# A hybrid RG-LRU and gating layer: an earlier end, statistics and splits spread over the boundaries, and three kinds of instruction pinned in order

## The chip, the cores and the metric

The kernel runs on one core of a Trainium2 chip. The metric is device time in microseconds (us), the median over runs; lower is better. Five engines with instruction lines of their own work on it: PE (matrix multiply), DVE (vector), ACT (scalar and activation), POOL and SP. DMA transfers are issued from SP's, ACT's and POOL's lines. An engine takes its instructions strictly in order.

## The reference, cut to what matters

```python
z = rms_norm(x, pre_g)                       # 2048 prompt tokens + 64 sample tokens, width 2048
proj = z @ w_in                              # width 5 * 1024: xr, gr, u, v, gs
xc, new_buf = causal_depthwise_conv(xr, ...) # 4 taps, with carried state for the samples
hr, h_last = rg_lru(xc, ...)                 # two gates per head (128 x 128), then h = a*h + b over time
br = hr * silu(gr)
v  = rms_norm(gelu(v), sgu_g)
bs = chunk_spatial_gating(gelu(u), v, w_s, b_s) * silu(gs)   # mixing inside chunks of 128 tokens
out = concat(br, bs) @ w_out                 # 2048 x 2048
y   = x + rms_norm(out, post_g)
```

All in float32. Outputs are y for prompt and samples, the new conv and recurrence states, and the normalised v of the samples.

## The kernel before, in words

**Groups.** The tokens are worked on in four groups of 512 prompt tokens; group 0 carries the 64 sample tokens with it (576 columns). Every product is taken as three passes of a split number: `split` (L155) makes a high half on ACT and a low half on DVE, and PE adds high·high, high·low and low·high. So each weight piece (128 x 1024) goes through three stations: a load `wraw` on SP's line (L176), its high half `wh` on ACT (L184), its low half `wl` on DVE (L192).

**Group 0** runs plain products, job by job: xr and gr for the recurrence (with conv, gates and scan, `lru0`, in between), v, gs and u, then sixteen out jobs, each a 128-row block of w_out. Its order on the engines is set by a scheduler; `later` (`tc.keep_in_program_order`, L92) ties one instruction to the place where the program hands it in. `at(job, f)` hands a task in behind a job. Beside it, in group 0, POOL's line loads quadrants of the weights (`load_quadrants`, L229) and `make_sums` (L236) forms four sums per unit (P1, P3, P2, P4), which are stored to memory: 16 units "c" of w_in on DVE, four of w_v and eight of w_or (from w_out) on POOL. At the end of the u jobs, `cat` is loaded again from memory as `cb` (L340) and split into c0h and c0l for the out jobs.

**Groups 1 to 3** use those sums for a scheme of seven products in place of eight: PROD names the weight side (B11, P4, B21, P2, P1, P3, B22), ACTS the activation side (A11, A22, A12, E, D1, D3, F, each with a high and a low half, `z_hi` on ACT and `z_lo` on DVE; `pre` forms E, D1, D3 and F before the split). A `quad` is two weight units for each of the seven products (14 steps), a `wide` four units (28 steps). Each group has four quads for xr and gr (G, 56 steps), one wide for v (V, 28), four quads for gs and u (U, 56) and two wides for out (O and R2, 28 each): 196 steps a group. Here the order is written by hand: `at2(s, f)` puts a task at step s, `early` ahead of it, `late` behind its matmuls. Loads run LOADS = 6 steps ahead, halves LOOK = 3, with three buffers each.

**Around the boundaries.** The next group's input x is loaded (`stat_load`), squared and summed on ACT (`stat_sum`), turned into 1/rms (`stat_rstd`), spread over the partitions by PE (`stat_spread` makes xd and the matmul nsx, L639; `stat_take` copies it back) and applied (`z_norm`). The finished group's output is normalised, x is added by an accumulating DMA on POOL's line, and stored (`finish_*`). For groups 1 and 2 four of eight quarters are still in the chip's memory and four are loaded again (`finish_load`, tile fo). At the very end the last group is done in halves of 256 rows: `last_rstd`, `last_gain`, then `last_scale` (ACT scales, a DMA accumulates into x, SP stores) for half 1 or `last_both` (DVE scales and adds, ACT stores) for half 0.

Of the kernel before, what the change touches and what calls it, by code (L numbers as in the profile page):

```python
# [46 lines left out]
PROD = ["B11", "P4", "B21", "P2", "P1", "P3", "B22"]  # L47
ACTS = ["A11", "A22", "A12", "E", "D1", "D3", "F"]


@with_exitstack
def hybrid_layer(ctx: ExitStack, tc: tile.TileContext, a):
# [183 lines left out]
    def make_sums(unit):  # L236
        nm = "_".join(str(x) for x in unit)
        t = state.pop(("quad", unit))

        def put(k, x):  # L240
            sums[unit, k] = hp.tile([P, W], F32, name=f"{k}_{nm}")
            side.dma_start(sums[unit, k], x)

        eng = nc.vector if unit[0] == "c" else nc.gpsimd
        eng.tensor_add(t["B11"], t["B11"], t["B12"])
        put("P1", t["B11"])
        eng.tensor_add(t["B12"], t["B12"], t["B22"])
# [402 lines left out]
    def z_norm(g, j, rows=(0, 1)):  # L650
        x = state["R", g, j]
        for i in rows:
            nc.vector.scalar_tensor_tensor(x[:, i, :TP], x[:, i, :TP], col(C_PRE, 2 * j + i), state["rB", g],
                                           op0=ALU.mult, op1=ALU.mult)

# [62 lines left out]

    def evac(r, bk, tmp, put):

        k = PROD[r]
        if k == "B11":
            nc.scalar.activation(tmp["U"], bk["a"], AF.Copy)
        elif k == "B21":
            put(0, 0, bk["a"], None, None)
        elif k == "P2":
            nc.vector.tensor_sub(tmp["U"], bk["b"], tmp["U"])
        elif k == "P1":
            nc.scalar.activation(tmp["D"], bk["d"], AF.Copy)
# [14 lines left out]
    def quad(g, name, unit_pairs, put):  # L744
# [21 lines left out]
    def wide(g, name, kind, q, put):  # L766

        bks, tmp = {}, {}

        def mm(r, u, key):  # L770
            b = BANK[PROD[r]]
            if u == 0 and b not in bks:
                bks[b] = [bank(f"w{g}{name}{b}{i}") for i in range(2)]
            mm_wide(key, r, u, bks[b])

        def take_product(r, i):
            if i == 0 and r == 0:
                tmp["U"] = dbl(f"U{g}{name}")
            elif i == 0 and PROD[r] == "P1":
                tmp["D"] = dbl(f"D{g}{name}")  # L780
            evac(r, {x: y[i] for x, y in bks.items()}, {x: y[:, i, :TP] for x, y in tmp.items()},
                 lambda n, half, *args: put(n, half, i, tmp, *args))

        for r, k in enumerate(PROD):
            for u in range(4):
                steps2.append((mm, r, u, (g, kind, q, u, k)))
            for i in range(2):
                at_once = k == "P1" or (k == "B22" and g == NG - 1 and name == "o1")
                early[len(steps2) + (0 if at_once else i)].append((take_product, r, i))

# [238 lines left out]

    def last_scale(half, qq):  # L1030

        o, x = state["og", half, qq], state["lx", half, qq]
        for i in range(2):
            nc.scalar.activation(o[:, i], o[:, i], AF.Copy, scale=state["lors", half][:, i:i + 1])
        side.dma_start(x, o, accum_op=ALU.add)
        nc.sync.dma_start(rows("y", NG - 1, half, qq), x)

    def last_both(half, qq):
# [3 lines left out]
        for i in range(2):  # L1042
            nc.vector.scalar_tensor_tensor(x[:, i], o[:, i], state["lors", half][:, i:i + 1], x[:, i],
                                           op0=ALU.mult, op1=ALU.add)
            nc.scalar.dma_start(y[:, i], x[:, i])

# [33 lines left out]
    for g in range(1, NG):  # L1080
# [98 lines left out]

    for c in ACTS:  # L1180
        for j in range(4):
            if c == "E":
                pre(("R", 1), "D3", j)
            if c in ("E", "D1", "F"):
                pre(("R", 1), c, j)
            z_hi(("R", 1), c, j)
            z_lo(("R", 1), c, j)

    def combine(key, c, j, s):

        at2(s, z_hi, key, c, j)
        at2(s + 1, z_lo, key, c, j)

    for g in range(1, NG):
        G = len(steps2)
        V, U, O, R2 = G + 56, G + 84, G + 140, G + 168
        for n, us in enumerate(XG):
            quad(g, f"xg{n}", us, put_xg(g, 2 * n))  # L1200
# [205 lines left out]
```

## Time and profile before

| | us |
|---|---|
| median of 3 runs (lowest to highest) | 2599.7 (2595.08 to 2603.26) |
| profiled execution, its own time | 2598.45 |
| its span in the trace | 2596.8 |
| PE busy | 2502.2 (96%) |
| DVE, ACT, POOL busy | 1737.8, 1398.3, 468.0 |
| mean granted PE clock | 0.988 |

In the rows below, a timeline line has start, duration, engine, source line, operation, out<-in, shape, a count, and in brackets the idle time before it with what ended it. L numbers are lines of the kernel before; in the changed kernel the same code stands 3 or more lines further down. Group 0 lasts to about 804 us, group 1 to about 1402, group 2 to about 1998. A tile's buffer numbers are left out in the profile (pB11c for all units "c").

### The profile page before, as it was taken

To read this page: it belongs to the slowest core of one execution; us is meant where nothing else is said; L and a number is where in the kernel's file an instruction comes from. 1 tells how busy PE (TensorE), PEld (TensorE's weight loads), DVE (VectorE), ACT (ScalarE), POOL (GpSimd) and SP (SyncE) were. 2 spreads that over 40 slices of the span, in tenths; PEclk is the share of its full clock that TensorE was granted. 3 is DMA by queue.
4 is the path that set the end of the run, shared out by engine and by line. 5 is a ranking of instruction groups with operands and counts; after the bars stand their busy time and mean duration, and the time that the engine had idled before them with its cause. 6 is when DMAs were issued, how large, how long until landed. Compare 5 with 4: busy or idle time off the path is not lost.

```text
span 2596.8 us, 41550 instructions
## 1 busy us (share of the span) xinstructions
PE 2502.2 (96%) x16710; PEld 2303.2 (89%) x16710; DVE 1737.8 (67%) x2236; ACT 1398.3 (54%) x1787; POOL 468.0 (18%) x552
## 2 busy tenths in 40 slices
PE   7989999999998999999999899999999899999996
PEld 6989789999997998899888898899878898899884
DVE  7776165554357786756788586656789587656865
ACT  5445332232144677555765577645756577645653
POOL 4331025954721200100100200000100200000000
PEclk9999999999999999999999999999999999999998
DMA  6995389975764855856876955555876955555676
GB/s 227 327 329 207 103 315 327 366 264 199 279 210 150 283 189 171 250 180 191 276 247 206 298 194 163 183 182 189 263 255 202 316 181 177 179 181 177 191 265 184
DMA packets 168673, 589.21 MB, mean 227 GB/s; under 512 B 19216, under 2 KB 19776, under 8 KB 168480
## 3 DMA queue, kind: packets, MB, share of 16 engines
q1 hardware_dynamic: 106544, 377.06, 43.7%
q0 software_dynamic: 60784, 207.40, 23.9%
q8 instruction: 130, 2.13, 0.3%
q10 hardware_dynamic: 1152, 2.10, 0.2%
q14 instruction: 63, 0.52, 0.1%
HBM read 494.92 MB, written 89.47 MB: 225 GB/s over the span
## 4 chain that ended last, share of the span: by engine, by line
PE 70%; DMA 9%; DVE 8%; ACT 5%; issue 5%; POOL 3%; SPq 0%; DVEq 0%; ACTq 0%; POOLq 0%
PE gm0v L378 4%; PE gm0gs L367 4%; PE gm0u L367 4%; PE gm0out L367 3%; PE gm0gr L367 3%; PE gm0xr L367 2%; DVE wl_c_B L192 1%; PE g L854 1%; PE sp L556 1%; DMA pB12c<-w_in 1%; DMA wraw_c_P<-P_c 1%; PE w3vd L713 1%; PE w2o1a L713 1%; PE w1o1d L713 1%; PE w3o1a L713 1%
## 5 line engine op out<-in xcount | busy, mean ns | idle before, releaser
L184 ACT ACTIVATE wh_c_P<-wraw_c_P 128x1024 fp32r<-128x1024 f32 x192 | 203.1, 1059 | 270.6 <-DMA wraw_c_P<-P_c 89.7
L192 DVE TENSOR_TENSOR wl_c_P<-wraw_c_P,wh_c_P 128x1024 fp32r<-128x1024 f32 x192 | 234.4, 1222 | 114.7 <-ACT wh_c_P L184 114.6
L192 DVE TENSOR_TENSOR wl_c_B<-wraw_c_B,wh_c_B 128x1024 fp32r<-128x1024 f32 x144 | 175.4, 1221 | 85.4 <-ACT wh_c_B L184 85.4
L184 ACT ACTIVATE wh_c_B<-wraw_c_B 128x1024 fp32r<-128x1024 f32 x144 | 152.0, 1057 | 140.3 <-DMA wraw_c_B<-w_in 41.6
L192 DVE TENSOR_TENSOR wl_w_or_P<-wraw_w_or_P,wh_w_or_P 128x1024 fp32r<-128x1024 f32 x96 | 117.4, 1223 | 44.5 <-ACT wh_w_or_P L184 44.1
L184 ACT ACTIVATE wh_w_or_P<-wraw_w_or_P 128x1024 fp32r<-128x1024 f32 x96 | 101.6, 1058 | 81.9 <-DMA wraw_w_or_P<-P_w_or 26.0
L184 ACT ACTIVATE wh_w_or_B<-wraw_w_or_B 128x1024 fp32r<-128x1024 f32 x72 | 76.2, 1059 | 80.4 <-DMA wraw_w_or_B<-w_or 24.5
L367 PE MATMUL gm0out<-c0l,wh_out 128*128 128x288 f32 x512 | 111.7, 299 | 1.0 <-DVE c0l L158 0.8
L367 PE MATMUL gm0out<-c0h,wl_out 128*128 128x288 f32 x512 | 110.5, 297 | 0.5 <-DVE wl_out L192 0.4
L367 PE MATMUL gm0out<-c0h,wh_out 128*128 128x288 f32 x512 | 110.4, 297 | 0.0
L192 DVE TENSOR_TENSOR wl_w_or_B<-wraw_w_or_B,wh_w_or_B 128x1024 fp32r<-128x1024 f32 x72 | 88.0, 1222 | 32.8 <-ACT wh_w_or_B L184 32.3
L617 POOL DMA_DIRECT2D xs<-xt x24 | 12.8, 536 | 504.7 <-ACT wh_c_P L184 257.3
L192 DVE TENSOR_TENSOR wl_out<-wraw_out,wh_out 128x1024 fp32r<-128x1024 f32 x32 | 48.2, 1507 | 64.4 <-ACT wh_out L184 64.4
L184 ACT ACTIVATE wh_out<-wraw_out 128x1024 fp32r<-128x1024 f32 x32 | 33.7, 1056 | 97.8 <-PE gm0out L367 66.7
L367 PEld LDWEIGHTS gm0out<-c0l,wh_out 128*128 128x128 f32 x512 | 82.4, 189 | 2.3 <-DVE c0l L158 1.7
L367 PEld LDWEIGHTS gm0out<-c0h,wl_out 128*128 128x128 f32 x512 | 82.4, 189 | 1.5 <-DVE wl_out L192 1.0
L367 PEld LDWEIGHTS gm0out<-c0h,wh_out 128*128 128x128 f32 x512 | 82.2, 189 | 0.1
L192 DVE TENSOR_TENSOR wl_w_v_P<-wraw_w_v_P,wh_w_v_P 128x1024 fp32r<-128x1024 f32 x48 | 58.5, 1222 | 28.5 <-ACT wh_w_v_P L184 28.5
L184 ACT ACTIVATE wh_w_v_P<-wraw_w_v_P 128x1024 fp32r<-128x1024 f32 x48 | 49.9, 1054 | 47.0 <-DMA wraw_w_v_P<-P_w_v 35.0
L367 PE MATMUL gm0gr<-z0h,wl_gr 128*128 128x288 f32 x256 | 56.9, 304 | 7.1 <-DVE wl_gr L192 7.1
L367 PE MATMUL gm0xr<-z0h,wh_xr 128*128 128x288 f32 x256 | 56.6, 302 | 7.2 <-ACT wh_xr L184 5.1
L378 PE MATMUL gm0v<-wh_v,z0l 128*128 128x512 f32 (+1 forms) x160 | 63.3, 396 | 0.0
(1612 smaller groups left out, 8610.8 us busy)
## 6 DMA issues: line engine op xcount, KB each, us to landing
wraw_c_P<-P_c SPq DMA_DIRECT2D x192, 512.0 KB, 4.1
wraw_c_B<-w_in SPq DMA_DIRECT2D x144, 512.0 KB, 4.2
wraw_w_or_P<-P_w_or SPq DMA_DIRECT2D x96, 512.0 KB, 4.2
wraw_w_or_B<-w_or SPq DMA_DIRECT2D x72, 512.0 KB, 4.1
wraw_w_v_P<-P_w_v SPq DMA_DIRECT2D x48, 512.0 KB, 3.6
wraw_w_v_B<-w_v SPq DMA_DIRECT2D x36, 512.0 KB, 3.3
wraw_out<-w_out SPq DMA_DIRECT2D x32, 512.0 KB, 4.5
xs<-xt POOLq DMA_DIRECT2D x24, 512.0 KB, 6.3
```

The source lines that it names most:

```text
L184: nc.scalar.activation(h[:, sl], raw[:, sl], AF.Copy)
L192: nc.vector.tensor_sub(l[:, sl], raw[:, sl], h[:, sl].bitcast(F32))
L367: nc.tensor.matmul(p[:, :n], w, zz[:, o:o + n], start=(k == 0 and n_pass == 0), stop=(k == KT - 1 and n_pass == 2))
L378: nc.tensor.matmul(p[:n], zz[:, c * P:c * P + n], w, start=(k == 0 and n_pass == 0), stop=(k == KT - 1 and n_pass == 2))
L556: nc.tensor.matmul(p[:, c * P:(c + 1) * P], state["vn", c, h // 4][:, vs], wst[:, h, :], start=True, stop=True)
L617: side.dma_start(x, a[f"xt{g}"][c * P:(c + 1) * P, b * W:(b + 1) * W])
L713: nc.tensor.matmul(bks[b], zz, w, start=(not cont and kk == 0 and n_pass == 0), stop=(kk == HALF - 1 and n_pass == 2), skip_group_check=True)
L854: nc.tensor.matmul(p, ww[:, ws], xx[:, i, :TP], start=n_pass == 0, stop=n_pass == 2)
```

## The change

Three parts.

*End.* The last wide takes its products in the order PROD_END (B11, P2, P4, P3, P1, B21, B22), with `evac` adapted, so rows 256 to 511 (half 1) are complete after the fifth product. `last_scale` is gone: `last_both` serves both halves; half 1 runs in steps R2 + 22 to R2 + 26 and stores on SP's line, half 0 stores alternately on ACT's and SP's.

*Boundaries.* Group 1's statistics move from the out jobs 8 to 11 to the out jobs 3 to 10, one task per job at the end. Before the first step of group 1 only A11 and A22 are split; A12, E, D1, D3 and F are split in steps 0 to 10. Finishing group 0 starts at step 14 in place of 4. Finishing groups 1 and 2: the four quarters in memory take every second step from G + 5; the four reloaded ones move from G + 5 .. 20 to V + 16 .. 36.

*Pins.* `later` is put around the first sum of every unit, group 1's squares and the first row of each z_norm of group 1.

```diff
+PROD_END = ["B11", "P2", "P4", "P3", "P1", "B21", "B22"]
...
-        eng.tensor_add(t["B11"], t["B11"], t["B12"])
+        later(eng.tensor_add(t["B11"], t["B11"], t["B12"]))
...
+        i = nc.scalar.activation(x, x, AF.Square, accum_out=state["xss", g][:, c, b:b + 1])
+        if g == 1:
+            later(i)
...
+        elif k == "P1" and end:
+            put(1, 1, bk["d"], tmp["D"], ALU.add)
...
+        elif k == "P3" and end:
+            nc.vector.tensor_sub(tmp["D"], tmp["U"], bk["c"])
+            put(0, 1, bk["e"], tmp["D"], ALU.subtract)
...
-        side.dma_start(x, o, accum_op=ALU.add)
-        nc.sync.dma_start(rows("y", NG - 1, half, qq), x)
...
-            nc.scalar.dma_start(y[:, i], x[:, i])
+            (nc.sync if half or qq % 2 else nc.scalar).dma_start(y[:, i], x[:, i])
...
-        at(("out", 8 + n // 4), stat_load, 1, n)
-        at(("out", 9 + n // 4), stat_sum, 1, n)
-    for f in (stat_rstd, stat_spread, stat_take):
-        at(("out", 11), f, 1)
+        at(("out", 3 + n // 2), stat_load, 1, n)
+        at(("out", 5 + n // 2), stat_sum, 1, n)
+    at(("out", 9), stat_rstd, 1)
+    at(("out", 10), stat_spread, 1)
+    at(("out", 10), stat_take, 1)
...
-    for c in ACTS:
+    for c in ("A11", "A22"):
         for j in range(4):
-            if c == "E":
-                pre(("R", 1), "D3", j)
-            if c in ("E", "D1", "F"):
-                pre(("R", 1), c, j)
             z_hi(("R", 1), c, j)
             z_lo(("R", 1), c, j)
+    for c in ("D3", "E", "D1"):
+        for j in range(4):
+            pre(("R", 1), c, j)
...
+    for j in range(4):
+        combine(("R", 1), "A12", j, j // 2)
+        combine(("R", 1), "E", j, 2 + j // 2)
+        combine(("R", 1), "D1", j, 4 + j // 2)
+        combine(("R", 1), "D3", j, 6 + j // 2)
+        at2(5 + j, pre, ("R", 1), "F", j)
+        combine(("R", 1), "F", j, 8 + j // 2)
...
-            at2(G + 8, load_gq, g - 1, 0)
+            at2(V + 16, load_gq, g - 1, 0)
             for n in range(4):
                 k = (g - 1, n % 2, n // 2)
-                at2(G + 5 + n, finish_load, *k)
-                at2(G + 11 + n, finish_scale, *k)
-                at2(G + 12 + n, finish_add, *k)
-                at2(G + 17 + n, finish_store, *k)
+                t = V + 21 + 3 * n
+                at2(t - 5, finish_load, *k)
+                at2(t, finish_scale, *k)
+                at2(t + 1, finish_add, *k)
+                at2(t + 6, finish_store, *k)
...
-    at2(R2 + 15, last_gain, 0, 2)
-    at2(R2 + 26, last_rstd, 1)
-    for qq in (2, 3):
-        at2(R2 + 26, last_gain, 1, qq)
+    at2(R2 + 18, last_gain, 1, 2)
+    at2(R2 + 22, last_rstd, 1)
+    at2(R2 + 22, last_gain, 1, 3)
     for qq in range(4):
-        at2(R2 + (27 if qq < 2 else 29), last_scale, 1, qq)
+        at2(R2 + 23 + qq, last_both, 1, qq)
+    at2(R2 + 26, last_gain, 0, 2)
```

Where the scheduler places the instructions of group 0 is not in the diff, so here are three places. First DVE's line in the recurrence of heads 0 and 1 (a, i, r, q belong to its gates, xc to its scan, wl_gr is the low half of a weight piece; the long numbers count tiles). Before:

```order
L481 SCALAR_TENSOR_TENSOR r_0_952<-q_0_1168,r_0_952 128x576
L487 MEMSET a_0_1162 128x1
L494 MEMSET a_0_1162 128x8
L245 TENSOR_TENSOR pB11c_0_1900<-pB11c_0_1900,pB12c_0_1902 128x1024
L481 SCALAR_TENSOR_TENSOR r_1_974<-q_1_1172,r_1_974 128x576
L487 MEMSET a_1_1165 128x1
L494 MEMSET a_1_1165 128x8
L247 TENSOR_TENSOR pB12c_0_1902<-pB12c_0_1902,pB22c_0_1904 128x1024
L486 MEMSET r_0_952 128x1
L486 MEMSET r_1_974 128x1
L249 TENSOR_TENSOR pB22c_0_1904<-pB22c_0_1904,pB11c_0_1900 128x1024
L488 TENSOR_TENSOR i_0_963<-i_0_963,r_0_952 128x576
```

The scan and wl_gr_1_1266 follow behind these rows. The changed kernel at the same place:

```order
L484 SCALAR_TENSOR_TENSOR r_0_952<-q_0_1168,r_0_952 128x576
L490 MEMSET a_0_1162 128x1
L497 MEMSET a_0_1162 128x8
L484 SCALAR_TENSOR_TENSOR r_1_974<-q_1_1172,r_1_974 128x576
L490 MEMSET a_1_1165 128x1
L497 MEMSET a_1_1165 128x8
L489 MEMSET r_0_952 128x1
L491 TENSOR_TENSOR i_0_963<-i_0_963,r_0_952 128x576
```

The three sums of a unit "c" have left this place.

Second, DVE at the start of group 1 (R1A, R1E, R1D are halves of activation sides, wl_c the low halves of the weight pieces that PE takes step by step). Before, 24 instructions stand between wl_c_0_P_8000 and the next wl_c; of them the first six:

```order
L192 TENSOR_TENSOR wl_c_0_P_8000<-wraw_c_0_P_7990,wh_c_0_P_7998 128x1024
L687 TENSOR_TENSOR R1A_0_7912<-xr_4_7505,R1A_0_7912 128x512
L687 TENSOR_TENSOR R1A_1_7915<-xr_5_7507,R1A_1_7915 128x512
L687 TENSOR_TENSOR R1A_2_7918<-xr_6_7633,R1A_2_7918 128x512
L687 TENSOR_TENSOR R1A_3_7921<-xr_7_7635,R1A_3_7921 128x512
L687 TENSOR_TENSOR R1E_7926<-xr_4_7505,R1E_7926 128x512
L687 TENSOR_TENSOR R1E_7931<-xr_5_7507,R1E_7931 128x512
```

The changed kernel:

```order
L195 TENSOR_TENSOR wl_c_0_P_7940<-wraw_c_0_P_7926,wh_c_0_P_7934 128x1024
L694 TENSOR_TENSOR R1A_0_7936<-xr_4_7263,R1A_0_7936 128x512
L694 TENSOR_TENSOR R1A_1_7938<-xr_5_7265,R1A_1_7938 128x512
L195 TENSOR_TENSOR wl_c_0_P_7977<-wraw_c_0_P_7928,wh_c_0_P_7969 128x1024
L694 TENSOR_TENSOR R1A_2_7973<-xr_6_7391,R1A_2_7973 128x512
L694 TENSOR_TENSOR R1A_3_7975<-xr_7_7393,R1A_3_7975 128x512
L195 TENSOR_TENSOR wl_c_0_B_8015<-wraw_c_0_B_7930,wh_c_0_B_8005 128x1024
L694 TENSOR_TENSOR R1E_8009<-xr_4_7263,R1E_8009 128x512
L694 TENSOR_TENSOR R1E_8011<-xr_5_7265,R1E_8011 128x512
```

Two splits now stand between two weight pieces.

Third, POOL's line around the reload of cat for the out jobs (u is a product of the gating branch, which the last c tiles need; P_w_or are stores of sums). Before, with the sums of w_or unit 1 long done:

```order
L549 TENSOR_TENSOR u_6_5551<-u_6_5551,gs_6_5277 128x576
L340 DMA cb_4_5712<-cat_4_2314 128x576
L340 DMA cb_5_5718<-cat_5_2328 128x576
L340 DMA cb_6_5724<-cat_6_3177 128x576
L340 DMA cb_7_5730<-cat_7_3191 128x576
L549 TENSOR_TENSOR u_7_5734<-u_7_5734,gs_7_5424 128x576
L340 DMA cb_8_5752<-cat_8_4224 128x576
```

The changed kernel, from u_6 to the third store:

```order
L552 TENSOR_TENSOR u_6_5551<-u_6_5551,gs_6_5277 128x576
L248 TENSOR_TENSOR pB11w_or_1_5362<-pB11w_or_1_5362,pB12w_or_1_5364 128x1024
L343 DMA cb_4_5712<-cat_4_2314 128x576
L245 DMA P_w_or_1_5557<-pB11w_or_1_5362 128x1024
L250 TENSOR_TENSOR pB12w_or_1_5364<-pB12w_or_1_5364,pB22w_or_1_5366 128x1024
L343 DMA cb_5_5718<-cat_5_2328 128x576
L245 DMA P_w_or_1_5560<-pB12w_or_1_5364 128x1024
L252 TENSOR_TENSOR pB22w_or_1_5366<-pB22w_or_1_5366,pB11w_or_1_5362 128x1024
L343 DMA cb_6_5724<-cat_6_3177 128x576
L245 DMA P_w_or_1_5563<-pB22w_or_1_5366 128x1024
```

The four sums of that unit stand between the reloads, ahead of cb_7, u_7 and cb_8.

More of the change, by code (lines that the diff above doesn't have):

```diff
@@ L48 @@
 ACTS = ["A11", "A22", "A12", "E", "D1", "D3", "F"]
+ACT_OF = dict(zip(PROD, ACTS))
+PROD_END = ["B11", "P2", "P4", "P3", "P1", "B21", "B22"]
 @with_exitstack
@@ L652, in z_norm @@
         for i in rows:
-            nc.vector.scalar_tensor_tensor(x[:, i, :TP], x[:, i, :TP], col(C_PRE, 2 * j + i), state["rB", g],
-                                           op0=ALU.mult, op1=ALU.mult)
+            n = nc.vector.scalar_tensor_tensor(x[:, i, :TP], x[:, i, :TP], col(C_PRE, 2 * j + i), state["rB", g],
+                                               op0=ALU.mult, op1=ALU.mult)
+            if g == 1 and i == 0:
+                later(n)
     def parts(key, j):
@@ L717, in hybrid_layer, with evac @@
     BANK = {"B11": "a", "P4": "e", "P2": "b", "B21": "a", "P3": "c", "P1": "d", "B22": "d"}
-    def evac(r, bk, tmp, put):
-        k = PROD[r]
+    def evac(k, bk, tmp, put, end=False):
         if k == "B11":
@@ L768, in wide, with mm, take_product @@
         bks, tmp = {}, {}
-        def mm(r, u, key):
-            b = BANK[PROD[r]]
+        end = g == NG - 1 and name == "o1"
+        def mm(k, u, key):
+            b = BANK[k]
             if u == 0 and b not in bks:
[L773 to L777, printed above, removed]
+                bks[b] = [(aux if end and b == "d" else bank)(f"w{g}{name}{b}{i}") for i in range(2)]
+            mm_wide(key, k, u, bks[b])
+        def take_product(k, i):
+            if i == 0 and k == "B11":
                 tmp["U"] = dbl(f"U{g}{name}")
-            elif i == 0 and PROD[r] == "P1":
+            elif i == 0 and k == ("P3" if end else "P1"):
                 tmp["D"] = dbl(f"D{g}{name}")
-            evac(r, {x: y[i] for x, y in bks.items()}, {x: y[:, i, :TP] for x, y in tmp.items()},
-                 lambda n, half, *args: put(n, half, i, tmp, *args))
-        for r, k in enumerate(PROD):
+            evac(k, {x: y[i] for x, y in bks.items()}, {x: y[:, i, :TP] for x, y in tmp.items()},
+                 lambda n, half, *args: put(n, half, i, tmp, *args), end)
+        for k in PROD_END if end else PROD:
             for u in range(4):
-                steps2.append((mm, r, u, (g, kind, q, u, k)))
+                steps2.append((mm, k, u, (g, kind, q, u, k)))
             for i in range(2):
-                at_once = k == "P1" or (k == "B22" and g == NG - 1 and name == "o1")
-                early[len(steps2) + (0 if at_once else i)].append((take_product, r, i))
+                at_once = k == "P1" or (k == "B22" and end)
+                early[len(steps2) + (0 if at_once else i)].append((take_product, k, i))
     def take(dst, ps, other, op, func=None):
@@ L1019, in last_gain @@
         o = state["fin", NG - 1, half, qq][:, :, :Q]
-        t = zlo.tile([P, 2, Q], F32, tag="zE", name=f"og{half}_{qq}") if away else o
+        t = zhi.tile([P, 2, Q], F32, tag="zA22", name=f"og{half}_{qq}") if away else o
         nc.vector.tensor_mul(t, o, gq(qq).unsqueeze(1).to_broadcast([P, 2, Q]))
@@ L1086, in add_wide @@
         def add_wide(kind, q):
-            for k in PROD:
+            for k in PROD_END if (g, kind, q) == (NG - 1, "w_or", 1) else PROD:
                 for u in range(4):
@@ L1278, in hybrid_layer @@
                 at2(O + 5 + 3 * n // 2, stat_sum, g + 1, n)
-            at2(O + 18, stat_rstd, g + 1)
-            late[O + 19].append((stat_spread, g + 1))
-            at2(O + 20, stat_take, g + 1)
+            at2(O + 17, stat_rstd, g + 1)
+            late[O + 20].append((stat_spread, g + 1))
+            at2(O + 21, stat_take, g + 1)
             for j in range(8):
@@ L1316, in hybrid_layer @@
         at2(R2 + 29, last_both, 0, qq)
-    late[4].append((norm_a, "o"))
-    late[7].append((norm_b, "o"))
+    late[8].append((norm_a, "o"))
+    late[14].append((norm_b, "o"))
     base = pos_of[steps2[0][3]]
```

33 lines of the change are left out of this document (15 added, 18 removed).

## The prediction, made before the changed kernel was run

> **What bounds the kernel now.** I read the page first, then the waits of PE, then the windows around the large waits, then DVE's timeline in each of them.
>
> ```profile
> PE 2502.2 (96%) x16710; PEld 2303.2 (89%) x16710; DVE 1737.8 (67%) x2236; ACT 1398.3 (54%) x1787; POOL 468.0 (18%) x552
> ```
>
> PE is busy for 2502.2 of 2596.8 us, and the change takes no matmul away. So only 94.6 us are open: its idle time, plus what it computes at half clock. Who holds it, from the waits of PE (total, times, longest):
>
> ```profile
> PE q1xg0e L699 <- DVE wl_c_P L192: 7.7, 1, 7.7
> PE gm0gr L367 <- DVE wl_gr L192: 7.1, 2, 4.4
> PE q3xg0d L699 <- DVE wl_c_B L192: 4.1, 2, 3.9
> PE q2xg0d L699 <- DVE wl_c_B L192: 3.9, 2, 3.7
> PE nsx L639 <- DVE xd L634: 3.8, 1, 3.8
> PE q1xg0e L699 <- ACT wh_c_P L184: 2.4, 1, 2.4
> PE gm0out L367 <- DVE c0l L158: 0.8, 1, 0.8
> ```
>
> The first six hold seven stalls of over 2 us, 28.5 us in sum (4.39 + 2.68 + 3.76 + 2.38 + 7.74 + 3.67 + 3.86). In each, PE waits for something small that stands late in DVE's or ACT's line. The windows show what follows a stall (length, PE busy, PE loads, DVE, ACT, POOL, granted clock, DMA share, GB/s):
>
> ```profile
> 130.00:140.00 10.00, 5.61 (x31) 5.37 (x30) 10.00 (x20) 3.60 (x4) 3.13 (x6) 0.83 0.85 279
> 745.00:755.00 10.00, 6.24 (x32) 5.00 (x31) 7.68 (x9) 1.25 (x3) 4.63 (x6) 0.83 0.91 330
> 815.00:825.00 10.00, 4.30 (x20) 4.30 (x21) 7.91 (x11) 2.44 (x4) 1.35 (x3) 0.51 0.58 174
> 1035.00:1045.00 10.00, 8.31 (x29) 6.09 (x28) 8.27 (x11) 4.45 (x5) 1.44 (x2) 0.83 0.61 171
> 1435.00:1445.00 10.00, 6.33 (x40) 6.13 (x39) 7.18 (x13) 3.70 (x4) 2.20 (x3) 0.75 1.06 345
> ```
>
> A mean clock of 0.83 over 10 us is 3.4 us at half speed, which loses up to 1.7 us of work; 0.75 is 5 us, 2.5 lost. At 815 the 0.51 is nearly the whole window at half speed, but PE worked in only 4.3 us of it, so 2.1 are lost. So a stall here costs its length and about 1.3 to 2.5 more.
>
> **The change, part by part.** Sums are against the profiled execution, 2598.45 us (span 2596.8, and 1.65 around it); the median of the runs, 2599.7, is 1.25 above.
>
> *First weight sums pinned (group 0).* DVE around the first two wl_gr stalls, PE's stall between them:
>
> ```profile
> 124.79 1.22 DVE L245 TENSOR_TENSOR pB11c<-pB11c,pB12c 128x1024 f32<-128x1024 f32 x1 [4.42 <-DMA pB12c<-w_in]
> 126.63 1.22 DVE L247 TENSOR_TENSOR pB12c<-pB12c,pB22c 128x1024 f32<-128x1024 f32 x1
> 134.00 1.20 DVE L192 TENSOR_TENSOR wl_gr<-wraw_gr,wh_gr 128x1024 fp32r<-128x1024 f32 x1
> 135.25 0.53 PE L367 MATMUL gm0gr<-z0h,wl_gr 128*128 128x288 f32 x2 [4.39 <-DVE wl_gr L192]
> 175.26 1.23 DVE L245 TENSOR_TENSOR pB11c<-pB11c,pB12c 128x1024 f32<-128x1024 f32 x1 [2.88 <-DMA pB12c<-w_in]
> 180.62 1.22 DVE L192 TENSOR_TENSOR wl_gr<-wraw_gr,wh_gr 128x1024 fp32r<-128x1024 f32 x1
> ```
>
> DVE stands 4.42 us before a sum whose quadrant has not landed, then does three sums (3.67 us), and only then the scan and wl_gr. Without them wl_gr would run about 8.1 us earlier, at 126; PE wanted it at 130.9 (135.25 − 4.39). The second runs 2.88 + 2.45 earlier (the wait and two sums), near 175.3; PE wanted it at 179.2, since its wait of 2.7 ended with wl_gr at 181.8. Both stalls go: 7.07, and 1.7 of clock. The sums do not vanish; the order puts them between later pieces, from the xr job just behind this wl_gr to the v jobs, one to four at a time. Gain 8.8. Bounds: 0, if another sum stands before the same wl_gr, to 9.5.
>
> *Statistics of group 1 spread over the out jobs.*
>
> ```profile
> 748.46 2.03 DVE L634 TENSOR_TENSOR xd<-ident,xrt 128x512 f32<-128x512 f32 x1
> ```
>
> Statistics, spread and take stood in one job, so PE reached nsx while xd was still behind a wl_out. Now the statistics close one whole job before the spread. All of 3.76 goes, with 1.2 of clock (half speed overlaps 2.4 us of work). Squares and loads come earlier by several jobs; the pin keeps ACT from running them ahead of their loads. Gain 5.0, bounds 2 to 5.
>
> *Boundary from group 0 to group 1.* DVE there:
>
> ```profile
> 802.58 1.23 DVE L192 TENSOR_TENSOR wl_c_P<-wraw_c_P,wh_c_P 128x1024 fp32r<-128x1024 f32 x1 [0.18 <-ACT wh_c_P L184]
> 803.72 3.75 DVE L687 TENSOR_TENSOR R1A<-xr,R1A 128x512 fp32r<-128x512 f32 x4
> 807.39 2.48 DVE L687 TENSOR_TENSOR R1E<-xr,R1E 128x512 fp32r<-128x512 f32 x4
> 809.80 4.89 DVE L687 TENSOR_TENSOR R1D<-xr,R1D 128x512 fp32r<-128x512 f32 x8
> 814.61 2.48 DVE L676 TENSOR_TENSOR xr<-xr 128x512 f32<-128x512 f32 x4
> 817.02 2.48 DVE L687 TENSOR_TENSOR R1F<-xr,R1F 128x512 fp32r<-128x512 f32 x4
> 819.43 1.21 DVE L192 TENSOR_TENSOR wl_c_P<-wraw_c_P,wh_c_P 128x1024 fp32r<-128x1024 f32 x1
> ```
>
> Between two weight pieces stand 24 instructions, 15.7 us in all; ACT has the matching row of high halves, which gives the 2.38 us wait. The change puts two splits between successive pieces: 1.22 + 2 × 0.62 = 2.5 us in a step of about 3.0 (588 steps share the 1785 us from 812 to the end), and 3.1 in the four steps that also prepare F. That just fits, so small waits of some tenths can stay. Stall 10.12 and clock 2.1 go; I leave 2 for the tight steps. Gain 10.2, bounds 5 to 12.2.
>
> *Finishing of the group before (g1→g2, g2→g3).*
>
> ```profile
> 1436.62 0.69 DVE L158 TENSOR_TENSOR wgl<-wg,wgh 128x512 fp32r<-128x512 f32 x1 [2.29 <-ACT wgh L157]
> 1438.51 1.41 DVE L1003 SCALAR_TENSOR_TENSOR fo<-fo,ors,gq 128x512 f32<-128x512 f32 x2 [1.20 <-DMA gq<-post_g]
> 1439.84 1.22 DVE L192 TENSOR_TENSOR wl_c_B<-wraw_c_B,wh_c_B 128x1024 fp32r<-128x1024 f32 x1
> ```
>
> The four reloaded quarters (gq, fo) move to the v stage, so wl_c_B can follow wgl at 1437.2 and not at 1439.84: 2.5 of 3.67 goes, and a stall of about 1 stays for wgh. With 2.5 of clock that is 5.0. The second boundary has the same form (3.86, and 3.4 us at half clock of which PE worked 2.6): 2.9 + 1.3. Gain 9.2, bounds 3 to 11.3. In the v stage the moved work adds four pairs of 0.70 us a group to DVE and a reload, an accumulation and a store for each; I take 1.5 for both groups, bounds 0 to 4, as weight pieces are just in time there too (the 1.7 us stall behind the 1035 window).
>
> *POOL at the first out job.* Here the pins cost. The sums of w_or unit 1, which stood before u_4, are now tied behind u_6 and stand between the reloads cb_4 to cb_7, ahead of u_7 and cb_8:
>
> ```profile
> 574.85 1.44 POOL L549 TENSOR_TENSOR u<-u,gs 128x576 f32<-128x576 f32 x1 [10.12 <-ACT u L548]
> 576.24 2.18 POOL L340 DMA_DIRECT2D cb<-cat  x4
> 586.22 1.89 POOL L549 TENSOR_TENSOR u<-u,gs 128x576 f32<-128x576 f32 x1 [7.80 <-ACT u L548]
> 588.06 3.22 POOL L340 DMA_DIRECT2D cb<-cat  x6
> L245 POOL TENSOR_TENSOR pB11w_or<-pB11w_or,pB12w_or 128x1024 f32<-128x1024 f32 x8 | 19.2, 2399 | 18.4 <-DMA pB12w_or<-w_or 18.3
> ```
>
> Four sums of 2.40, and four stores and four reload issues of 0.54 (2.18 for four) are 13.9 us from 576.3: POOL reaches u_7 at 590.2 and cb_8 at 592.1, 4 us late. PE takes the c halves one after another and waits 0.8 for one of them already, so I take a 3 us stall and 1 of clock: −4. Bounds 0 (the c tiles had slack) to −6.
>
> That last 1 of clock is a choice. [...]
>
> *The end.*
>
> ```profile
> 2570.91 1.39 DVE L796 TENSOR_TENSOR U3o<-w3o1d,U3o 128x512 f32<-128x512 f32 x2
> 2579.07 1.41 DVE L1043 SCALAR_TENSOR_TENSOR lx<-og,orsl,lx 128x512 f32<-128x512 f32 x2
> 2575.88 15.46 ACTq L1045 DMA_DIRECT2D y<-lx x8
> GB/s 0 0 8 0 0 0 0 0 0 0 0 0 172 186 172 203 190 211 371 338 201 227 262 295 295 293 272 291 281 385 369 387 379 389 131 0 0 8 0 0
> y<-lx ACTq DMA_DIRECT2D x8, 256.0 KB, 6.5
> ```
>
> PE's last matmul ends at about 2571.4, between the two U3o of the first row; 25.4 us remain. (The GB/s row has slices of 1 us from 2560.) DVE is through at 2580.5, but 6.3 MB of accumulation and stores move at 170 to 390 GB/s until 2594, and the last 2.8 us carry nothing. The new order of products finishes half 1 two products early and adds x on DVE; behind PE only half 0's 2.1 MB stay. The last store is issued at 2580.5, lands 3.6 (shortest of such stores) to 6.5 (median, in the crowd) later, and with 2.8 the end is 2586.9 to 2589.8: gain 7.0 to 9.9, I take 8.5. Half 1's chain now runs under PE (rstd, gain and eight scalings in five steps); the heaviest step holds about 4 us of DVE (rstd 1.6, gain 1.2, a low half 1.2) against 3.0, and two steps pass before PE needs that low half. Bounds 5 to 10.
>
> The stores of half 0 alternate between ACT's and SP's queue. [...]
>
> **Sum.** 8.8 + 5.0 + 10.2 + 9.2 − 1.5 − 4 + 8.5 = 36.2. 2598.45 − 36.2 = 2562.2, and 1.25 more for the median: 2563.5, say 2564.
>
> **Rivals.**
>
> *Half of the stalls come back elsewhere.* For it: the DVE line is full in the tight steps, and the waits list has 25 smaller ones of 0.2 to 1. Against: POOL and DVE have idle time nearby. Boundary terms halved (10.2 + 9.2 → 9.7), the v cost doubled (−3), POOL's term −6: 8.8 + 5 + 9.7 − 3 − 6 + 8.5 = 23, so 2577.
>
> *POOL's line holds everything (slower).* POOL is in order; the pinned first sum waits for its quadrants (18.3 us over eight, in the row above), and behind it stand cb, u, wg and the next quadrants. It decides if these holds reach PE. Eight w_or and four w_v units with their sums and stores (4 × 2.94 = 11.8 us each) are 141 us of POOL; where a third of that falls on PE's path (47 us), it takes the 36 and 11 more: 2611. Against: before u it idles 10.12 and 7.80, and it is busy for 18% of the span.
>
> *The pins do not hold.* If the sums only trade places, with other sums before wl_gr, the group-0 term is 0 and POOL's stays: 2598.45 − 27.4 + 1.25 = 2572.
>
> *Only the end pays.* If the boundaries are bound by weight loads (DMA share 1.06 at 1435), the stalls stay under other names: 8.5 + 5 − 4 = 9.5, so 2590.
>
> **Chances.** Forecast (2555 to 2572) 0.53; half returns 0.20; pins do not hold 0.08; only the end pays 0.07; slower 0.06; within no change 0.06, between the last two cases. A measurement of this kernel tells 0.3% (8 us) from nothing. Faster 0.88, same 0.06, slower 0.06. The range, 2552 to 2588, takes in the second and third cases; below, the sum with no residue and no POOL term (36.2 + 7.5 = 43.7, so 2556) and a full gain at the end.
>
> **What would show it.** Right: no wait of PE for wl_gr over 1 us between 120 and 200; none over 2 at nsx; at the first q1xg0 steps PE waits under 1 us each and the clock stays near 1; q2xg0d and q3xg0d wait about 1; the span ends some 17 us behind the last matmul. A PE stall at c0l near 590 of 2 to 4 us would confirm POOL's term. Wrong: a new wait of PE over 4 us anywhere, above all for wl pieces in the v stage or in the last two products, or an end still over 22 us behind PE.

## The result, and the profile after

| | before | after |
|---|---|---|
| median (lowest to highest) of 4 runs, us | 2600.1 (2595.1 to 2603.3) | 2571.1 (2567.2 to 2574.6) |
| ratio, 95% interval | | 0.9886, 0.9870 to 0.9903 |
| profiled execution, its span | 2598.45, 2596.8 | 2573.34, 2571.6 |
| PE busy, mean granted clock | 2502.2, 0.988 | 2502.0, 0.990 |

The change gains 29 us of 2600 (2564 was forecast, 2571 came). First the head of the page of the changed kernel:

```profile
PE 2502.0 (97%) x16710; PEld 2303.7 (90%) x16710; DVE 1758.0 (68%) x2244; ACT 1390.4 (54%) x1777; POOL 468.8 (18%) x548
```

Then the waits of PE (total, times, longest), as shown of the kernel before:

```profile
PE gm0out L370 <- DVE c0l L161: 6.5, 3, 4.5
...
PE q2ug0a L706 <- DVE wl_c_B L195: 3.6, 2, 3.2
PE q3ug0a L706 <- DVE wl_c_B L195: 3.6, 2, 3.2
PE sp L559 <- DVE s L565: 3.5, 1, 3.5
...
PE w1vb L720 <- DVE wl_w_v_P L195: 2.4, 2, 1.7
PE q1xg1d L706 <- DVE wl_c_B L195: 2.4, 1, 2.4
PE w1vb L720 <- ACT wh_w_v_P L187: 2.3, 2, 2.0
PE q3ug0a L706 <- ACT uw3ug L729: 1.7, 1, 1.7
```

All seven stalls that the prediction listed are gone: wl_gr twice, nsx, the two at q1xg0e, q2xg0d and q3xg0d. In their place stand new ones: at the first out job (c0l and sp, 9.7 us between 582 and 603), at the start of the u stage of groups 2 and 3 (wl_c_B, 3.2 us each, and 1.7), and in group 1's v stage (w1vb).

Where the time went is best read by stage. For each stage this is the distance between the first starts of PE's first tile of it and of the next stage, from the grouped view of PE's instructions of both profiled executions:

| stage | before | after | moved | the prediction's term |
|---|---|---|---|---|
| xr, gr (recurrence) | 251.4 | 243.8 | −7.6 | −8.8 |
| v, gs, u of group 0 | 329.4 | 329.4 | 0 | 0 |
| out jobs | 215.6 | 221.8 | +6.2 | −5.0 + 4 |
| group 1, first quads | 188.1 | 175.3 | −12.8 | −10.2 |
| group 1, v | 86.6 | 92.5 | +5.9 | 0 |
| groups 2 and 3, first quads | 180.5 + 178.9 | 169.1 + 169.7 | −20.6 | −9.2 |
| groups 2 and 3, v and u | 83.5 + 165.4 + 83.1 + 164.0 | 85.2 + 170.9 + 83.9 + 172.8 | +16.8 | +1.5 |
| behind PE's last matmul | 25.2 | 13.7 | −11.5 | −8.5 |

The rest (four stages of 157 to 166 us and the start) moved by −1.6 in sum. Together this is the 25.2 us between the spans; the medians are 29 apart, since the profiled execution of the changed kernel was 2.3 slower than its median, and that of the kernel before 1.6 faster.

The end, in DVE's timeline, then the DMA view from 2535 (bars of 1 us) of the changed kernel:

```profile
2565.36 1.41 DVE L1048 SCALAR_TENSOR_TENSOR lx<-og,orsl,lx 128x512 f32<-128x512 f32 x2
```

```profile
GB/s 66 324 143 147 332 45 160 360 4 0 0 0 61 328 285 373 303 215 371 162 201 324 0 0 0 0 0 0 365 309 244 348 399 252 184 4 0 0 8 0
...
y<-lx SPq DMA_DIRECT2D x12, 256.0 KB, 3.4
...
y<-lx ACTq DMA_DIRECT2D x4, 256.0 KB, 3.1
```

PE ends at 2557.9, DVE's last scaling at 2566.8, the last bytes land about 2570. Behind PE stand only half 0's stores; the stores of y land in a median of 3.4 us from SP's line and 3.1 from ACT's, where ACT's stores before took a median of 6.5.

### The profile page after: what moved, and what is told of

Read it like the earlier page. It is cut to its first block, busy times and chain, and to the rows that moved or that the text cites. A ratio compares the mean times of both kernels' runs of the same rounds, so it can differ in the third digit from the quotient of the medians.

```text
span 2571.6 us, 41575 instructions
## 1 busy us (share of the span) xinstructions
PE 2502.0 (97%) x16710; PEld 2303.7 (90%) x16710; DVE 1758.0 (68%) x2244; ACT 1390.4 (54%) x1777; POOL 468.8 (18%) x548
## 4 chain that ended last, share of the span: by engine, by line
PE 77%; DVE 7%; DMA 6%; ACT 5%; issue 4%; POOL 1%; SPq 0%; DVEq 0%; ACTq 0%; POOLq 0%
PE gm0out L370 8%; PE gm0v L381 4%; PE gm0gr L370 4%; PE gm0gs L370 4%; PE gm0u L370 3%; PE gm0xr L370 3%; DMA wraw_c_B<-w_in 1%; DMA wraw_w_v_P<-P_w_v 1%; PE g L866 1%; PE sp L559 1%; DVE wl_c_B L195 1%; DMA wraw_c_P<-P_c 1%; PE w1o0d L720 1%; PE w3o0d L720 1%; PE w2o1a L720 1%
## 5 line engine op out<-in xcount | busy, mean ns | idle before, releaser
L195 DVE TENSOR_TENSOR wl_out<-wraw_out,wh_out 128x1024 fp32r<-128x1024 f32 x32 | 63.6, 1987 | 35.7 <-ACT wh_out L187 35.6
L431 POOL DMA_DIRECT2D wg<-w_g x16 | 12.0, 747 | 390.7 <-ACT xch L850 129.3
## 6 DMA issues: line engine op xcount, KB each, us to landing
wraw_c_P<-P_c SPq DMA_DIRECT2D x192, 512.0 KB, 4.0
wraw_c_B<-w_in SPq DMA_DIRECT2D x144, 512.0 KB, 3.9
wraw_w_or_P<-P_w_or SPq DMA_DIRECT2D x96, 512.0 KB, 4.0
wraw_w_or_B<-w_or SPq DMA_DIRECT2D x72, 512.0 KB, 3.4
wraw_w_v_P<-P_w_v SPq DMA_DIRECT2D x48, 512.0 KB, 3.8
wraw_w_v_B<-w_v SPq DMA_DIRECT2D x36, 512.0 KB, 3.4
wraw_out<-w_out SPq DMA_DIRECT2D x32, 512.0 KB, 5.9
xs<-xt POOLq DMA_DIRECT2D x24, 512.0 KB, 6.3
```

The source lines that it names most:

```text
L195: nc.vector.tensor_sub(l[:, sl], raw[:, sl], h[:, sl].bitcast(F32))
L431: side.dma_start(w2.rearrange("p (h c) -> p h c", h=2), a["w_g"][hp_:hp_ + 2].rearrange("h p a c -> p h (a c)"))
```

## The experiments

### The end alone, and the pins alone

The kernel before with one part of the change each.

```diff
 e1: the kernel before + PROD_END, evac's end forms, last_both for both halves, stores on SP
 e2: the kernel before +
-        eng.tensor_add(t["B11"], t["B11"], t["B12"])
+        later(eng.tensor_add(t["B11"], t["B11"], t["B12"]))
     and the same around group 1's squares and the first row of its z_norm
```

> The kernel before with the first part of the change alone (new order of the last products, half 1 finished under PE, no accumulating DMA at the end). Theory: the end is set by the bytes behind PE's last matmul; the tail goes from 25.4 us to about 14, as in the changed kernel (13.9), and nothing else moves: 11.5 us faster, about 2588.5. The prediction's own term would be 8.5 (2591.5). Rival: the tail shortens, but half 1's work under PE costs PE stalls in the last two products of over 4 us: 2595 or more.

> The kernel before with the pins alone (first sum of every unit, group 1's squares, first row of its z_norm). Theory: both waits of PE for wl_gr go (7.1 us and the clock), and the w_or sums now stand between the cb reloads, where c0l comes late: some 9 us of PE waits for c0l and sp around 590. So the gain is nearly eaten: between 3 us faster and 3 slower, about 2600. Rival: the waits at c0l come from the earlier statistics (loads and squares in the out jobs), not from the pins: then 8 us faster, about 2592.

Measured: the end alone 2590.3 us, ratio 0.9959 (0.9944 to 0.9974), 10 us faster; its tail is 13.7 us and no wait of PE in the last products is new. The pins alone 2600.5 us, ratio 0.9999 (0.9985 to 1.0014). Its recurrence stage is 244.5 us (251.4 before) and its out jobs 223.4 (215.6): what the pins win at wl_gr they lose at the first out job. Two waits of its PE:

```profile
PE gm0out L367 <- DVE c0l L158: 6.4, 3, 4.5
...
PE sp L556 <- DVE s L562: 3.5, 1, 3.5
```

These are the two waits of the changed kernel to a tenth, so the pins make them and the earlier statistics do not.

### The boundaries alone

```diff
 the kernel before + the statistics, split and finishing steps of the change, without a pin
```

> The kernel before with the second part of the change alone (statistics of group 1 earlier, splits spread over steps 0 to 10, finishing moved). Theory: the three parts add up; the change gains 29 us, the end alone 10 and the pins alone 0, so this is 19 us faster than before, about 2581. Rival: the squares and scalings need their pins; free, the scheduler puts them where ACT or DVE wait for loads in front of weight pieces, and the gain is under 12 us (2588 or more).

Measured: 2579.2 us, ratio 0.9923 (0.9902 to 0.9944), 21 us faster. The parts add up within their uncertainty: 10 + 0 + 21 = 31 against 29. The out jobs take 209.2 us there, 6.4 less than before, so the statistics paid more than the predicted 5.0. The rival, that squares and scalings need their pins, falls: the same stage with these pins takes 209.1 us (the next experiment).

### Which pins cost: POOL's

```diff
-        later(eng.tensor_add(t["B11"], t["B11"], t["B12"]))
+        first = eng.tensor_add(t["B11"], t["B11"], t["B12"])
+        if unit[0] == "c":
+            later(first)
```

> The changed kernel, with the first sum pinned only for the 16 units that DVE adds; the units that POOL adds are free, and w_or unit 1 is summed ahead of u_5 again. Theory: the three PE waits at the first out job (1.8, 3.5 and 4.5 us) and about 2 us of half clock go: 9 to 11 us faster than the changed kernel, about 2561. Rival: the sums only take DVE's time elsewhere in the u jobs or hold the quadrant loads, and waits of the same size come at wl_gs or wl_u: within 3 us of the changed kernel.

Measured: 2555.4 us, ratio to before 0.9830 (0.9797 to 0.9863): 45 us faster than before, 16 faster than the changed kernel, more than the 9 to 11 expected. The out jobs fall from 221.8 to 209.1 us, the recurrence stage by 1.9. (The 12.7 us come again in the kernels further below: 221.8 in e4, which keeps these pins, 209.7 in e6 and e7, which do not have them.) The rival, that the waits move to the u jobs, falls: v, gs and u of group 0 take 329.4 us again.

### Why they cost: a late issue, or two engines in each other's way

In the changed kernel DVE's instructions are long at that place. Its DVE timeline, then POOL's and ACT's:

```profile
568.70 10.85 DVE L161 TENSOR_TENSOR c0l<-cb,c0h 128x576 fp32r<-128x576 f32 x4 [1.84 <-ACT c0h L160]
579.47 4.00 DVE L195 TENSOR_TENSOR wl_out<-wraw_out,wh_out 128x1024 fp32r<-128x1024 f32 x1
583.40 1.41 DVE L161 TENSOR_TENSOR c0l<-cb,c0h 128x576 fp32r<-128x576 f32 x2
...
585.87 0.45 DVE L400 TENSOR_TENSOR u<-gm0u,rsBx 128x288 f32<-128x288 f32 x1
...
593.50 2.31 DVE L161 TENSOR_TENSOR c0l<-cb,c0h 128x576 fp32r<-128x576 f32 x1 [2.67 <-ACT c0h L160]
595.73 3.99 DVE L195 TENSOR_TENSOR wl_out<-wraw_out,wh_out 128x1024 fp32r<-128x1024 f32 x1
```

```profile
569.07 2.91 POOL L248 TENSOR_TENSOR pB11w_or<-pB11w_or,pB12w_or 128x1024 f32<-128x1024 f32 x1
...
573.05 2.41 POOL L250 TENSOR_TENSOR pB12w_or<-pB12w_or,pB22w_or 128x1024 f32<-128x1024 f32 x1
...
576.54 2.38 POOL L252 TENSOR_TENSOR pB22w_or<-pB22w_or,pB11w_or 128x1024 f32<-128x1024 f32 x1
...
579.98 2.40 POOL L254 TENSOR_TENSOR pB21w_or<-pB21w_or,pB22w_or 128x1024 f32<-128x1024 f32 x1
582.32 0.57 POOL L343 DMA_DIRECT2D cb<-cat  x1
...
588.15 1.40 POOL L552 TENSOR_TENSOR u<-u,gs 128x576 f32<-128x576 f32 x1 [4.66 <-ACT u L551]
...
592.76 2.43 POOL L248 TENSOR_TENSOR pB11w_or<-pB11w_or,pB12w_or 128x1024 f32<-128x1024 f32 x1
```

```profile
575.57 0.69 ACT L160 ACTIVATE c0h<-cb 128x576 fp32r<-128x576 f32 x1 [3.58 <-DMA cb<-cat]
...
587.38 0.68 ACT L551 ACTIVATE u<-u 128x576 f32<-128x576 f32 x1 [4.20 <-DVE u L400]
```

The same four c0l took 3.54 us before. The wl_out that starts at 579.47 ends at 583.47, about a microsecond after the sum of 579.98 to 582.38 that it met; the c0l of 593.50 ends at 595.81, 0.6 us after the sum of 592.76 to 595.19. And u_7 at 588 did not stand behind the sums on POOL's line: POOL had been free for 4.66 us and waited for ACT, and ACT for a product of DVE (L400), which came late behind DVE's long instructions. The first of the new stalls, which ends at 584.2, is for the fifth c0l (583.40). ACT had its high half at 576.26; the long c0l and the wl_out ahead of it on DVE's line made it late, not the issue of its cb. But that c0h had itself waited 3.58 us for its cb, and the next ones waited too. So two mechanisms stand against each other, and two kernels were made to part them.

```diff
 e5, in make_sums, for the w_or units 1 and 2:
+            for k, b, z in (("P1", "B11", "B12"), ("P3", "B12", "B22"), ("P2", "B22", "B11"), ("P4", "B21", "B22")):
+                later(eng.memset(t[b], 0.0))
+                later(eng.memset(t[b], 0.0))
+                put(k, t[b])
 e10, where the sums are handed in:
-((45 + 20.5 * n, load_quadrants), (64 + 20.5 * n, make_sums))
+((45 + 20.5 * n, load_quadrants), (64 + 20.5 * n + (12.7 if u == ("w_or", 0, 1) else 0), make_sums))
```

> The changed kernel; for the two w_or units that POOL sums at the first out job, each of the eight sums is replaced by two fills with zeros of the same tile (so those weight sums are left out, and groups 1 to 3 use zeros for them). POOL is held about as long between the cb reloads, in the same order, but reads nothing. Theory A (the engines get in each other's way: DVE's two-input instructions run only when POOL's do not, as c0l x4 in 10.85 us against 3.54 before suggests): c0l takes 0.75 us again, and PE's waits for c0l and sp between 580 and 605 fall from 9.7 us to under 3. Theory B (the prediction's: POOL's line issues cb and u late): the waits stay at 7 to 10 us.

> The changed kernel with all its pins, but the sums of w_or unit 1 are handed in one out job (12.7 us of the program's own count) later, so that all cb reloads stand ahead of them on POOL's line. Theory A (POOL's two-input sums slow DVE's): the sums now run on from about 590, where c0l for the tiles 8 to 15 and two wl_out are made, so a part of the waits stays: PE waits of 3 to 6 us between 580 and 610 where the changed kernel has 10; 4 to 8 us faster than the changed kernel, about 2565. Theory B (only the late issue of cb and u counts): nothing stays; as e3, about 2556.

Measured, e5 (one execution): 2554.2 us. PE's waits at c0l are gone, and 2.1 us at sp remain; the out jobs take 211.2 us. c0l in e5 against the changed kernel (minimum/median/maximum ns, from the views of the tile c0l):

```profile
L161 DVE TENSOR_TENSOR c0l<-cb,c0h x14: 744/758/1496, 566.7 to 595.7; 128x576 fp32r<-128x576 f32 x14
```

```profile
L161 DVE TENSOR_TENSOR c0l<-cb,c0h x14: 744/746/3558, 568.7 to 604.6; 128x576 fp32r<-128x576 f32 x14
```

The first is e5, the second the changed kernel. Beside POOL's fills c0l takes 0.75 us; the maximum of 1.5 falls beside u_7's two-input product. But e5 is not quite clean: a fill takes 0.97 us and a sum 2.4, so cb_7 was issued 5.7 us after the end of u_6 there and 13.2 in the changed kernel: the late issue was more than halved too.

e10 is the complement: no reload waits behind a sum, but the sums run on beside c0l and wl_out. 2560.5 us, ratio to before 0.9844 (0.9826 to 0.9862), 10 us faster than the changed kernel where 4 to 8 were expected; out jobs 215.1:

```profile
PE gm0out L370 <- DVE c0l L161: 4.7, 2, 2.4
```

With the issue on time, 4.7 us of waits at c0l stay, inside the 3 to 6 that the theory of two engines gave; the theory of the late issue alone, which gave none, falls. Of the 12.7 us between the changed kernel and e3 in the out jobs, 6.0 (215.1 against 209.1) are there without any late issue, from sums that stand a little later. The other 6.7 go when the sums leave the reloads; how much of them is DVE's slowness on the earlier c0l, and how much the issue itself, is not parted further.

### What the finishing costs in its new place

```diff
 e4: the changed kernel, the reloaded quarters
-                t = V + 21 + 3 * n
+                t = G + 22 + 8 * n          # gq at G + 14
 e6, e7: e3 without finish_add, or without finish_scale, for these quarters
 e8: e3 with
-                t = V + 21 + 3 * n
+                t = V + 6 + 5 * n           # gq at V + 1; load 4 ahead, store 5 behind
 and group 0's sixteen pieces at 14 + 4 * j
```

> The changed kernel, with the four reloaded quarters of the finished group (load, scale, accumulate, store) spread at steps 22, 30, 38 and 46 of the next group's first stage in place of 21 to 30 steps into its v stage. Theory: the PE waits at the first u quad of groups 2 and 3 (3.2 us each, 1.7 more, and their clock), and the slower v stage behind them, come from the weight loads that are late behind this traffic (DMA share 0.9 to 1.1 there, 0.4 to 0.7 at the new place): 12 to 16 us faster than the changed kernel, about 2557. Rival: any 1.4 us of DVE in a step is too much, and the same waits come in the first stage: within 3 us of the changed kernel.

> The kernel without pins on POOL's sums (e3, 2555.4 us), with the accumulating DMA of x left out for the four reloaded quarters of groups 1 and 2 (so y lacks x there). Theory: the PE waits at the first u quad (2.0 and 2.8 us, with their clock) come from weight loads that are late behind this traffic; without a third of it they fall under 1 us, and v and u stages of groups 2 and 3 together fall from 504.3 us to 498: about 2549. Rival: DVE's four scalings per group are what is late: no change (2554 to 2557).

> As e6, but the scalings on DVE are left out for these quarters and the accumulating DMA stays (so y lacks 1/rms and gain there). Theory (traffic): the waits at the first u quad stay, 2554 to 2557. Rival (DVE): they go, about 2549.

> e3 (no pins on POOL's sums) with the finishing spread thinner: group 0's sixteen pieces every 4 steps from step 14 of group 1, and the four reloaded quarters of groups 1 and 2 at steps 6, 11, 16 and 21 of the v stage, gq one stage earlier. Theory: the waits in group 1's v stage (7 us in sum there) and at the first u quads (4.8 us) come from traffic in bursts; spread, they fall by half: 6 to 10 us faster than e3, about 2547. Rival: the output tiles hold buffers that the gates of the first stage need, as in e4 (ACT waited for a store of y there): equal or slower, 2555 to 2565.

Measured, e4: 2588.4 us, ratio to before 0.9952 (0.9938 to 0.9967), 17 us slower than the changed kernel. The v and u stages of groups 2 and 3 are clean (83.1 + 164.9 + 82.8 + 164.1 = 494.9 us against 512.8), so it is this work that costs there. But the first quads grow by 18.7 and 19.9 us. PE waits about 13 and 14 us in them, most of it for weight pieces, as the rival said; the longest single waits, 5.4 and 5.1 us, are of a kind that neither theory named. They are for a gate (the total over the run, then what ACT waited for from 1400 to 1580):

```profile
PE g L866 <- ACT r L872: 10.8, 3, 5.4
```

```profile
ACT i L872 <- DMA y<-fo: 2.9, 1, 2.9
...
ACT L872 <- DMA y<-fo: 1.9, 1, 1.9
```

The gate's tiles r and i are taken from the pool of 13 buffers from which fo comes, and ACT waits until a store of y has let go of one: 1.9 us ahead of the r that PE waited 5.4 for, 2.9 ahead of an i. So held buffers are a part of the price of this work; how large a part of the 19 us a group isn't parted.

e6 (one execution, y without x in these quarters): 2556.0 us, its v and u stages 507.4 against 504.3 in e3. e7 (one execution, without the scalings): 2560.8, and 512.0. Neither helps, so neither the accumulating transfers nor DVE's scalings alone make the late weights. In e7, where no scaling paces them, the transfers start in a burst; its transfers from 1600 to 1650 (median us to landing), and those of e4 at the same stage, where they are absent:

```profile
wraw_w_v_P<-P_w_v SPq DMA_DIRECT2D x3, 512.0 KB, 9.6
fo<-xt POOLq DMA_DIRECT2D x3, 512.0 KB, 13.1
```

```profile
wraw_w_v_P<-P_w_v SPq DMA_DIRECT2D x8, 512.0 KB, 3.6
```

A weight piece lands in 9.6 us in the burst and in 3.6 without it, and the v stage of group 2 takes 90.5 against 83.1. That fits traffic that makes loads late, but it is a coincidence of rows; e6, with a sixth of the bytes less (10.77 MB against 12.83 in e3 from 1605 to 1650), should then have gained something and did not: its c pieces (wraw_c_P) landed in 4.1 us there against 6.1 in e3, and PE still waited 1.9 and 3.2 us at the first u quads (2.0 and 2.8 in e3). A fourth buffer for raw weight pieces would be a direct test; it wasn't tried. The cause stays open.

e8: 2568.1 us, ratio 0.9854 (0.9818 to 0.9891). That is 13 us slower than e3 by the medians and 6 by the ratios, whose intervals overlap; it is not the 6 to 10 faster of the theory. The v stages of groups 2 and 3 become 92.8 and 88.4, their u stages 165.6 and 164.9, in sum 511.7 against 504.3 in e3: the cost went where the work went, once more. Group 1's first quads take 6.1 us more (180.7) and its v stage 5.1 less (86.4). No place that was tried takes this work for nothing.

**The fastest.** e3 beats both kernels: 2555.4 us, 0.9830 of before, by taking the pins off the sums that POOL makes.

## Why the prediction was right, and where it was not

The forecast of 2564 (2552 to 2588) held the measured 2571; the first rival's number, 2577, is as near. In part that is luck. By the spans the change gained 25.2 us where the sum had 36.2: POOL's term was 8.7 too good, the finishing 9.8, and the other terms together were 7.4 too low. The medians lie 29 apart and not 25 because of where the two profiled executions fell. By its steps:

- *First sums pinned.* Right: no wait for wl_gr is left, and the stage is 7.6 us shorter against 8.8 forecast.
- *Statistics.* Right in mechanism, low in size: 6.4 us in the boundaries alone, against 5.0. A part of the old stall was something the prediction did not see: xd took 2.03 us in the row it quoted, where its minimum in the same kernel is 0.69, beside a two-input instruction of POOL (748.52 to 749.93).
- *POOL at the first out job.* The step that failed. Its place and its sign were right, its sum was 4 us and the runs showed 12.7. It counted the late issue of cb and u_7 (13.9 us of POOL's line), and had no term for DVE's own instructions getting longer. The runs showed that beside POOL's sums a c0l takes up to 3.6 us and a wl_out 4.0, with PE waiting 9.7 us and then working at a clock of 0.79 to 0.86. The late u_7, on which the working rested, was not late on POOL's line but behind ACT and DVE, as the rows above show. Not parted, as said, are 6.7 of the 12.7 us.

The windows of the changed kernel there, columns as in the prediction:

```profile
570.00:580.00 10.00, 10.00 (x76) 9.81 (x75) 10.00 (x4) 3.93 (x6) 9.95 (x10) 1.00 0.53 177
580.00:590.00 10.00, 4.77 (x28) 4.16 (x26) 9.90 (x10) 2.25 (x4) 5.29 (x5) 0.79 0.80 270
590.00:600.00 10.00, 7.95 (x47) 7.30 (x46) 7.33 (x5) 5.19 (x8) 9.95 (x13) 0.86 0.89 281
600.00:610.00 10.00, 7.28 (x43) 7.29 (x44) 8.28 (x10) 0.69 (x1) 2.03 (x1) 0.83 0.47 160
```

From 570 to 580 DVE is busy all the time with 4 instructions: that row is how it looks here when c0l, 0.75 us in e5, takes up to 3.6 beside POOL's sums.

- *Boundary from group 0 to group 1.* Right, and a little better: 12.8 against 10.2; the 2 us left for tight steps were not needed at the boundary, since q1xg0's steps show no wait at all. One of 2.4 us came 80 us on, at q1xg1d.
- *Finishing moved.* Both sides were mis-sized. The gain was 20.6 against 9.2, because the prediction took only the stall at q2xg0d and q3xg0d, kept 1 us of it, and left out the later ones of the same stage (the wait of g for ACT's r of 2.4 at 1477 among them), which went too. The cost was 16.8 against 1.5 in the v and u stages, and 5.9 in group 1's v stage, which the sum didn't hold at all, though the change puts nine of group 0's sixteen pieces there where six stood before. The prediction priced the moved work as pairs of 0.70 us on DVE and took 1.5 us for both groups, with 4 as the upper bound; that step failed too. The stalls show ACT waiting for weight pieces instead:

```profile
1655.94 1.06 ACT L187 ACTIVATE wh_c_B<-wraw_c_B 128x1024 fp32r<-128x1024 f32 x1 [3.19 <-DMA wraw_c_B<-w_in]
```

What in the moved work makes them late is open (above). Net, −20.6 + 16.8 + 5.9 is +2.1 us, against −7.7 forecast: errors of opposite sign, 11 and 21 us, that cancel in part. This execution lies at the upper end: in e3, e5, e9 and e10, which keep these steps of the finishing, the v and u stages of groups 2 and 3 take 504 to 507 us, 8 to 11 above the 496.0 before, and their first quads 340 to 344 (359.4 before). With group 1's v stage (91.5 to 93.3) the move gains 2 to 4 us net there, still less than the forecast.
- *The end.* Right in mechanism, 11.5 against 8.5 in the traces and 10 in the medians of the end alone. The size missed on the landing time: 3.1 to 3.4 us with a third of the bytes, below the 3.6 that was the lower end; and about 1.6 us behind the last bytes carry nothing, where 2.8 were counted.
- *The 1 us of clock in the POOL term* can't be judged at that place: it was counted for one stall of 3 us, and the first two stalls there (1.8 and 3.5 us) are only 0.4 us of work apart and share one stretch at a lower clock (0.79 over 10 us), and the third is 4.5 us long. Single, shorter stalls elsewhere tell more, and they differ. The changed kernel behind its stall of 2.35 us at q1xg1d, then the kernel before behind its stall of 2.68 us at wl_gr:

```profile
886.00:896.00 10.00, 10.00 (x73) 10.00 (x74) 8.44 (x14) 4.91 (x6) 2.61 (x5) 0.83 0.94 257
```

```profile
182.00:192.00 10.00, 10.00 (x76) 10.00 (x77) 10.00 (x23) 5.12 (x6) 3.18 (x6) 1.00 0.94 345
```

So a stall of 2.35 us was followed by a lower clock, as the prediction took it, and one of 2.68 us was not: in these traces the length alone does not say if the clock falls. The prediction, whose windows left the second one out, gave a price in clock to the first stall at wl_gr alone, and that was right.
- *The second store queue.* Landing fell about as much for SP's twelve stores as for ACT's four (medians 3.4 and 3.1 us, 6.5 for ACT's eight before); no run parts the queues from the bytes.

Of the signs named beforehand as wrong, one came: a new wait of PE over 4 us, the 4.5 at c0l.

## What to carry to other kernels

Where two engines can take the same kind of work, look at what the neighbour's instruction takes beside it, not only at who stands in line: an engine that is busy all the time with few instructions in a window (here DVE with 4 in 10 us) may be held, and the same instruction's time elsewhere tells (c0l 10.85 us for four, 3.54 before). An order pinned for one engine's sake should be pinned for that engine alone; here the same one-line pin won 8 us on DVE's units and lost 13 on POOL's. And before moving background work, price what it holds (buffers, the landing time of the loads beside it) besides what it computes; in each of the three new places where it was tried, this work cost 4 to 20 us a group.

## What the runs showed of the hardware

- In the changed kernel two-input instructions of DVE took longer beside two-input sums of POOL: c0l up to 3.6 us beside sums of 2.4 to 2.9, with a median of 0.75; the c0l of 593.50 took 2.31 and ended 0.6 us after the sum that it met. wl_out has a median of 1.23 and took up to 7.7, from 711.12, beside two sums and an accumulation of POOL between 711.02 and 717.76. Beside POOL's fills of 0.97 us no such stretch of c0l was seen (e5, median 0.76). The other way round, POOL's accumulation acco at 752.71 in the changed kernel took 5.76 us (1.41 the shortest) beside two-input instructions of DVE, among which wl_out took its usual 1.21.
- Not each of these cost PE time: it waited 1.8 and 4.5 us for a c0l in the changed kernel, and nowhere for the wl_out of 7.7 us.
- A PE stall of 1.7 us was followed by a stretch at half clock in the kernel before (0.50 from 1041 to 1044), one of 2.35 us in the changed kernel too (0.83 over 10 us), and one of 2.68 us in the kernel before was not (1.00).
- A 512 KB load took 3.6 us (median of 8, e4) where POOL's queue moved nothing beside it, and 9.6 (median of 3, e7) in a burst of transfers on POOL's queue at the same stage.
